# Experts of a mixture-of-experts layer: four at a time in four column groups of the array, on unsplit fp32 weights

## The chip, the cores and the metric

One core of one Trainium2 chip runs the whole program in one launch. The metric is the device time of one execution in microseconds. Before the change the median of 3 runs is 1587.62 us (1587.09 to 1587.66). The profile is one further execution of the same kernel.

## What is computed

A small network on 256 tokens of width 1024, all in fp32. A first block has a mixer (gated linear attention and block attention), attention over a memory, and a mixture of experts; after it come two layers of another kind (differential and stick-breaking attention, then a feed-forward part). The change lies in the mixture of experts. Each token picks one of 4 groups, and in it 2 of 8 experts, so 32 experts share 512 token places:

```
hid = silu(xb @ w_gate[e]) * (xb @ w_up[e])
return (hid @ w_down[e]) * w[:, None]
...
out = zeros((T, D)).at[buf_t].add(yb)
```

Here xb are the tokens of expert e. w_gate and w_up are 32 x 1024 x 512, w_down is 32 x 512 x 1024: 6 MB of fp32 for an expert, 201.3 MB for all, and every byte is used once.

## The kernel before

Nearly all large products run on fp32 weights split into two parts of the type fp32r. A weight chunk is 128 partitions x 1024 elements (512 KB). `load` (line 276) issues its transfer from SP's queue, `high` (L286, instruction L288) rounds it to fp32r on ScalarE, and `low` (L291, instruction L293) takes the difference on VectorE, or now and then on GpSimd. In the other layers `dense` (L317) multiplies three combinations of high and low parts (L327).

The expert stage begins at L706 with the buffers. `raws` (L713) is a ring of places that hold chunks: 16 buffers of `moeraw`, the idle tiles `kTc`, `vc`, `hBl`, `hAl`, `hAh`, `hBh`, the four buffers of `wraw`, two of `Y` once, and `gain`. Loads are issued in program order; SP waits at each for its buffer. The first four chunks are requested while the product before the stage still runs (L812), the next 25 ahead of the stage (`EARLY`, L896), the rest as the stream consumes them.

The routing (L855 to L885) works on VectorE: largest values, their positions, and the place of each token in its expert's list of 32 slots. Between its operations the splits of the first chunks are issued (L794, and L868 and L869 with the low parts on GpSimd). `select` (L922) makes a 0/1 matrix of tokens and slots for four experts, and `take` (L928) multiplies the rows of x by it in fp32, which gives the chosen tokens transposed. `put` (L937) writes them as a high part on ScalarE and a low part on VectorE. Each expert has 64 columns: 32 slots of high part and 32 of low part; 128 stationary columns hold one expert and a zero block or the neighbour.

A unit is two experts. `up` (L1059) streams the chunks of gate and up weights: per chunk the high and the low split, then 2 x 2 matmuls of 128 x 512 (`parts`, L1010, instruction L1015). The high and low rows of the result are added up by a product with a constant matrix (`comb`, L1070), which also transposes it. `hidden` (L1072) applies the gate and splits again. `down` (L1093) streams the down weights the same way. `weights` (L1034) multiplies the selection by the routing weights on GpSimd (L1039) and transposes it, and `scatter` (L1101) adds the weighted rows back to x for two units at a time (L1106, L1110). The order of chunks is up(0), up(1), down(0), up(2), down(1), and so on to down(15). Side work is put on an agenda that is counted in chunks (`at`, `tick`, L907 to L916).

After unit 10 (`OVER`) comes a branch for experts with more than 32 tokens (`overflow`, L1133, the branch itself L1138). All engines go through it. Loads of some chunks are issued before it, into places that the branch doesn't use.

At the end the last units are added up in PSUM (`add`, L1128, L1131), the result is normed and transposed (L1234 to L1298), and the next layer starts with L327.

Of the kernel before, what the change touches and what calls it, by code (L numbers as in the profile page):

```python
# [20 lines left out]
P = 128  # L21
# [6 lines left out]
MOE_RAW = 16  # L28
LAG = 3
POOLED = (4, 24, 3)  # L30
EARLY = 25
PAST = 16
OVER = 10
GAINS = 8
SECOND = 7
SHARES = 8
WARM = (2, 4)
ADDS = 2
# [13 lines left out]
ADDX = (2, 5, 3, 7)  # L52
# [13 lines left out]
def make_consts():  # L66
# [13 lines left out]
    e, r = np.arange(64)[None, :] // 32, np.arange(64)[None, :] % 32  # L80
    cols["comb"] = ((s // 64 == e) & (s % 32 == r)).astype(f)
# [27 lines left out]
GROUPS = (("ident", "ones", "before", "comb", "slots", "index", "down_from", "order"), ("tri16", "bucket"),  # L109
# [5 lines left out]
def forward(ctx: ExitStack, tc: tile.TileContext, a: dict, out: bass.AP):  # L115
# [595 lines left out]
    around = places[:-1] + shared, places[-1:]  # L711
# [5 lines left out]
    def nextraw():  # L717

        return next(v for v in raws if not closing or v[0] is not big or v[1] in ("kTc", "vc"))

    wg, wu, wd = a["w_exp_gate"][0], a["w_exp_up"][0], a["w_exp_down"][0]
    ahead, ready = collections.deque(), collections.deque()

    def halved(i, h, eng=nc.vector):
        ready.append((h, low(first[i], h, KC, 512, keep, eng)))

    with tc.tile_pool(name="crossp", bufs=1, reuse_waits="tile") as cp:
# [56 lines left out]
        def feed_moe(src, t, half):  # L784
# [8 lines left out]
            if half and t == 0:  # L793
                halved(0, high(first[0], KC, 512, keep))  # L794
# [16 lines left out]
        first = []  # L811
        add_to_x(slices(oT), a["w_co"][0], feed_moe, lambda: first.extend(  # L812
            load([wg[0, k0 * P:(k0 + KC) * P, :]], KC, 512, *nextraw()) for k0 in range(0, KD, KC)))
# [54 lines left out]
    for i in range(1, 4):  # L868
        halved(i, high(first[i], KC, 512, keep), nc.gpsimd)  # L869
# [18 lines left out]
    UNITS = [(2 * u, 2 * u + 1) for u in range(16)]  # L888
    last = len(UNITS) - 1
    xs2 = []  # L890
    for u in range(2):
        xs2.append(new(mp, [P, KD, 3, 2, 32], F32R, name="xs%d" % u))
        if u == 0:
            wt = s3("wt", 32)
            upcoming = [W[e, k0 * P:(k0 + KC) * P] for i in range(2) for e in UNITS[i] for W in (wg, wu) for k0 in range(0, KD, KC)]
            ahead.extend(load([src], KC, 512, *nextraw()) for src in upcoming[len(first):][:EARLY])  # L896
    hs2 = []
    for v in xs2:
        nc.gpsimd.memset(v[:, :, 1].bitcast(F32), 0.0)
    comb = cst("comb")  # L900
# [21 lines left out]
    def select(u):  # L922

        sel = sels[u] = new(mp2, [P, NT, 4, 32], name="sel")
        keep(tt(sel, key[:, :, 2 * u:2 * u + 4].rearrange("p t (e o) -> p t e o", o=1).to_broadcast([P, NT, 4, 32]),  # L925
                slots[:, None, None, :].to_broadcast([P, NT, 4, 32]), op=ALU.is_equal))

    def take(u, k0):  # L928

        ps = new(pst, [P, 4, 2, 2, 32], name="tp")  # L930
        for k in range(4):
            for t in range(NT):
                keep(mm(ps[:, k].rearrange("p u e r -> p (u e r)"), xr[:, t, (k0 + k) * P:(k0 + k + 1) * P],
                        sels[u][:, t].rearrange("p e r -> p (e r)"), start=(t == 0), stop=(t == NT - 1)))
        return ps

    def put(k0, ps, units=(0, 1)):  # L937
        views = [(xs2[i][:, k0:k0 + 4, 0::2], ps[:, :, i]) for i in units]
        for v, src in views:
            keep(nc.scalar.copy(v[:, :, :, 0], src))  # L940
        for v, src in views:
            keep(tt(v[:, :, :, 1], src, v[:, :, :, 0].bitcast(F32), op=ALU.subtract))

    def gather(u, first, step, lag):
        select(u)
        for i in range(2):
            at(first + step * i, lambda k0: at(lag, put, k0, take(u, k0)), 4 * i)
# [62 lines left out]
    def parts(xf, e, nk, last, acc, W, col):  # L1010

        def go(k0, ww):
            for i in range(2):
                for k in range(KC):
                    keep(mm(acc, xf[:, k0 + k, e * 64:e * 64 + P], ww[i][:, k],  # L1015
                            start=(e == 0 and k0 == 0 and i == 0 and k == 0),
                            stop=(e == last and k0 + KC == nk and i == 1 and k == KC - 1)))

        return [(W[k0 * P:(k0 + KC) * P, col:col + 512], functools.partial(go, k0)) for k0 in range(0, nk, KC)]

    def stream(chunks):
        for src, go in chunks:
            if ready:
                go(ready.popleft())
            else:
                raw = ahead.popleft() if ahead else load([src], KC, 512, *nextraw())
                h = high(raw, KC, 512, keep)
                go((h, low(raw, h, KC, 512, keep, nc.gpsimd if clock[0] < POOLED[1] and clock[0] % POOLED[0] == POOLED[2] else nc.vector)))
            tick()

    def flat(v):
        return v.rearrange("p k a b c -> p k (a b c)")

    def weights(u):  # L1034

        sel = sels[u - u % 2][:, :, u % 2 * 2:u % 2 * 2 + 2]
        selw = new(mp2, [P, NT, 2, 2, 32], name="selw")
        for d in range(2):
            nc.gpsimd.tensor_tensor(selw[:, :, :, d], sel,  # L1039
                                    wt[:, :, 2 * u:2 * u + 2].rearrange("p t (e o) -> p t e o", o=1).to_broadcast([P, NT, 2, 32]),  # L1040
                                    op=ALU.mult)
        ps = new(psm, [P, 512], name="mm")

        def turn():
            for t in range(NT):
                nc.tensor.transpose(ps[:, t * P:(t + 1) * P], selw[:, t].rearrange("p e d r -> p (e d r)"), ident)
            at(LAG, read)

        def read():
            sT[u] = new(mp, [P, T], name="selT", bufs=4)  # L1050
            keep(nc.scalar.copy(sT[u], ps[:, 0:T]))

        at(2, turn)

    def up_chunks(u, G=None, U=None):
        return [c for e, x_ in enumerate(UNITS[u]) for acc, W in ((G, wg), (U, wu))
                for c in parts(flat(xs2[u % 2]), e, KD, len(UNITS[u]) - 1, acc, W[x_], 0)]

    def up(u):  # L1059

        G, U = new(psm, [P, 512], name="mm"), new(psm, [P, 512], name="mm")
        at(2 if u else PAST, weights, u)
        stream(up_chunks(u, G, U))
        gu = [new(tmp, [P, 512], name="rows") for _ in range(2)]
        ps = new(psm, [P, 2, 4, 64], name="mm")

        def read(i, v):
            keep(nc.scalar.copy(gu[i], v))
            for k in range(4):
                keep(mm(ps[:, i, k], gu[i][:, k * P:(k + 1) * P], comb, start=True, stop=True))  # L1070

        def hidden():  # L1072
            if u < 2:
                hs2.append(new(mp, [P, 4, 3, 2, 32], F32R, name="hs%d" % u))
                nc.gpsimd.memset(hs2[u][:, :, 1].bitcast(F32), 0.0)
            hs = hs2[u % 2]
            hid = new(mp2, [P, 4, 64], name="hid")
            keep(nc.scalar.activation(hid, ps[:, 0], AF.Sigmoid))
            keep(nc.vector.tensor_mul(hid, hid, ps[:, 0]))
            keep(nc.vector.tensor_mul(hid, hid, ps[:, 1]))  # L1080
            hv = hid.rearrange("p k (e r) -> p k e r", e=2)
            keep(nc.scalar.copy(hs[:, :, 0::2, 0], hv))
            keep(tt(hs[:, :, 0::2, 1], hv, hs[:, :, 0::2, 0].bitcast(F32), op=ALU.subtract))

        at(LAG - 4, read, 0, G)
        at(LAG, read, 1, U)
        at(LAG + 2, hidden)

    def down_chunks(u, Y=(None, None)):
        return [c for e, x_ in enumerate(UNITS[u]) for half in range(2)  # L1090
                for c in parts(flat(hs2[u % 2]), e, 4, len(UNITS[u]) - 1, Y[half], wd[x_], half * 512)]

    def down(u):  # L1093

        Y = [new(psa, [P, 512], name="at") for _ in range(2)]
        stream(down_chunks(u, Y))
        Yg[u] = new(mp, [P, 2, 512], name="Y", bufs=2)
        for half in range(2):
            at(LAG - 2 + 2 * half, lambda *v: keep(nc.scalar.copy(*v)), Yg[u][:, half], Y[half])

    def scatter(units, first, step, lag):  # L1101
        def piece(t, half):
            hs = slice(half * 512, (half + 1) * 512)
            ps = new(pst, [P, 512], name="tp")
            for i, u in enumerate(units):
                mm(ps, sT[u][:, t * P:(t + 1) * P], Yg[u][:, half], start=(i == 0), stop=(i == len(units) - 1))  # L1106
# [447 lines left out]
```

## Time and profile before

| What | Value |
|---|---|
| median of 3 runs | 1587.62 us |
| the profiled execution's own time | 1591.64 us |
| its span, first to last instruction | 1590.0 us |
| mean granted TensorE clock | 0.989 |
| PE busy | 1532.9 us (96%), 7099 instructions |
| DVE busy | 1190.1 us (75%), 1498 instructions |
| ACT busy | 992.1 us (62%), 1353 instructions |
| POOL busy | 199.8 us (13%), 95 instructions |
| read from HBM | 381.10 MB |

The page lists busy times of the engines, then the span in 40 slices of 39.75 us, the queues of transfers, the chain that ended last, and groups of like instructions. PE is the TensorE matmul, PEld its weight load, DVE is VectorE, ACT ScalarE, POOL GpSimd, and SPq the queue from which SP issues loads. Matmul ends are modelled and overlap, so a busy PE is not a PE at its peak; distances between starts say more. In rows of the timeline the columns are the start in us, the duration in us, the engine, the line, the operation, the output and inputs, the shape, the count, and in brackets the idle time before and what ended it.

### The profile page before, as it was taken

The page shows a single profiled execution, that of the slowest core. Times are in us where ns is not written, and L with a number is a line of the kernel's source. Part 1 is how long each engine was busy: PE and PEld are TensorE (multiplying, and loading weights), DVE is VectorE, ACT ScalarE, POOL GpSimd, SP SyncE. Part 2 cuts the span into 40 slices and gives each one's busy share as a digit, 9 for nine tenths or more (in the row PEclk, how much of TensorE's full clock was granted, in tenths as well). Part 3 has the DMA queues.
Part 4 walks back from the last instruction along what each step waited for, and adds up shares of the span by engine and source line. Part 5 has one row for each costly group of instructions (what it writes and reads, how often), then busy time and mean ns, then how long its engine had stood idle before and what let it go on. Part 6 is the DMA issues. An engine that isn't in the chain of part 4 may idle for free. (4 is left out here: it accounts for less than half of the span.)

```text
span 1590.0 us, 20604 instructions
## 1 busy us (share of the span) xinstructions
PE 1532.9 (96%) x7099; PEld 1194.5 (75%) x7099; DVE 1190.1 (75%) x1498; ACT 992.1 (62%) x1353; POOL 199.8 (13%) x95
## 2 busy tenths in 40 slices
PE   7999999699999999999999999999999999999998
PEld 5778887466776767767667887888888887888886
DVE  5665575789999999999887876766656876766654
ACT  5455554579878887797774666555544566455543
POOL 1110000434335141142001000000000000000000
PEclk9999999899999999999999999999999999999999
DMA  8645559689999999999956545566567545566653
GB/s 283 218 137 160 182 173 375 209 295 370 386 387 387 386 387 340 341 386 386 387 187 195 147 141 164 182 189 186 185 186 220 168 137 152 178 195 186 184 187 106
DMA packets 220348, 383.59 MB, mean 241 GB/s; under 512 B 13464, under 2 KB 60000, under 8 KB 219856
## 3 DMA queue, kind: packets, MB, share of 16 engines
q1 hardware_dynamic: 217584, 373.76, 70.2%
q0 software_dynamic: 1648, 6.84, 1.4%
q10 hardware_dynamic: 1008, 1.64, 0.3%
q8 instruction: 57, 0.93, 0.2%
q14 instruction: 51, 0.42, 0.1%
HBM read 381.10 MB, written 2.65 MB: 241 GB/s over the span
## 5 line engine op out<-in xcount | busy, mean ns | idle before, releaser
L293 DVE TENSOR_TENSOR wl<-raw,wh 128x1024 fp32r<-128x1024 f32 x599 | 718.0, 1227 | 239.6 <-ACT wh L288 226.1
L288 ACT ACTIVATE wh<-raw 128x1024 fp32r<-128x1024 f32 x606 | 624.0, 1057 | 303.2 <-PE mm L327 258.9
L1015 PE MATMUL mm<-wl,xs 128*128 128x512 f32 x512 | 186.4, 446 | 8.6 <-DVE wl L293 5.5
L1039 POOL TENSOR_TENSOR selw<-sel,wt 128x128 f32<-128x128 f32 x32 | 139.7, 4385 | 272.9 <-DVE sel L925 187.6
L1015 PE MATMUL mm<-wh,xs 128*128 128x512 f32 x512 | 164.0, 403 | 0.6 <-ACT wh L288 0.6
L1015 PEld LDWEIGHTS mm<-wl,xs 128*128 128x128 f32 x512 | 91.3, 192 | 66.2 <-DVE wl L293 32.8
L327 PE MATMUL mm<-wh,hAl 128*128 128x512 f32 x424 | 139.1, 409 | 0.0
L327 PE MATMUL mm<-wh,hAh 128*128 128x512 f32 x424 | 134.3, 397 | 2.7 <-ACT wh L288 2.7
L327 PE MATMUL mm<-wl,hAh 128*128 128x512 f32 x424 | 134.3, 398 | 0.0
L327 PE MATMUL mm<-wl,hBh 128*128 128x512 f32 x424 | 133.3, 394 | 0.0
L327 PE MATMUL mm<-wh,hBl 128*128 128x512 f32 x424 | 132.4, 393 | 0.1
L327 PE MATMUL mm<-wh,hBh 128*128 128x512 f32 x424 | 132.1, 393 | 0.0
L1015 PEld LDWEIGHTS mm<-wh,xs 128*128 128x128 f32 x512 | 97.0, 191 | 27.2 <-ACT wh L288 3.7
L1015 PE MATMUL at<-wl,hs 128*128 128x512 f32 x256 | 89.4, 430 | 7.9 <-DVE wl L293 7.9
L327 PEld LDWEIGHTS mm<-wh,hAh 128*128 128x128 f32 x424 | 79.3, 190 | 19.8 <-ACT wh L288 3.1
L1015 PE MATMUL at<-wh,hs 128*128 128x512 f32 x256 | 87.2, 422 | 5.4 <-ACT wh L288 5.3
L327 PEld LDWEIGHTS mm<-wl,hAh 128*128 128x128 f32 x424 | 79.4, 190 | 17.2
L327 PEld LDWEIGHTS mm<-wh,hBh 128*128 128x128 f32 x424 | 78.9, 188 | 17.6
L327 PEld LDWEIGHTS mm<-wh,hBl 128*128 128x128 f32 x424 | 78.5, 188 | 18.0 <-issue 1.4
L327 PEld LDWEIGHTS mm<-wl,hBh 128*128 128x128 f32 x424 | 78.5, 188 | 16.9 <-issue 0.3
L327 PEld LDWEIGHTS mm<-wh,hAl 128*128 128x128 f32 x424 | 75.3, 191 | 12.3 <-issue 0.8
L1015 PEld LDWEIGHTS at<-wl,hs 128*128 128x128 f32 x256 | 45.1, 188 | 34.9 <-DVE wl L293 21.9
(482 smaller groups left out, 2245.5 us busy)
## 6 DMA issues: line engine op xcount, KB each, us to landing
raw<-in_w_in_dram SPq DMA_DIRECT2D x121, 512.0 KB, 3.7
raw<-in_w_exp_down_dram SPq DMA_DIRECT2D x101, 512.0 KB, 10.8
raw<-in_w_exp_gate_dram SPq DMA_DIRECT2D x95, 512.0 KB, 10.8
raw<-in_w_exp_up_dram SPq DMA_DIRECT2D x93, 512.0 KB, 10.8
raw<-in_w_ffn_in_dram SPq DMA_DIRECT2D x176, 256.0 KB, 3.2
raw<-in_w_ffn_out_dram SPq DMA_DIRECT2D x44, 512.0 KB, 3.8
raw<-in_w_out_dram SPq DMA_DIRECT2D x24, 512.0 KB, 3.8
raw<-in_w_ckv_dram SPq DMA_DIRECT2D x8, 512.0 KB, 3.9
```

The costliest lines, as they stand in the source:

```text
L288: order(nc.scalar.activation(h[:, :kc], raw[:, :kc], AF.Copy))
L293: order(eng.tensor_sub(l[:, :kc], raw[:, :kc], h[:, :kc].bitcast(F32)))
L327: order(mm(ps[t][:, :n], xs[k0 + k][part][:, t * P:(t + 1) * P], ww[:, k, :n], start=(k0 == 0 and i == 0 and k == 0), stop=(k0 + kc == nk ...
L1015: keep(mm(acc, xf[:, k0 + k, e * 64:e * 64 + P], ww[i][:, k], start=(e == 0 and k0 == 0 and i == 0 and k == 0), stop=(e == last and k0 + K ...
L1039: nc.gpsimd.tensor_tensor(selw[:, :, :, d], sel, wt[:, :, 2 * u:2 * u + 2].rearrange("p t (e o) -> p t e o", o=1).to_broadcast([P, NT, 2, ...
```

## The change

Four experts are worked on at once, each in 32 of the array's 128 columns, with the unsplit fp32 weights times 32 unsplit slots. The split of expert weights, their low parts on VectorE and GpSimd, the high and low slots, and the product with `comb` go. For gate and up weights a partition now takes two neighbouring rows (a 4 KB run) where it took two rows that lie 128 apart (two runs of 2 KB), and `take` picks the columns of x to match; for down weights a chunk is 128 whole rows of 4 KB, but in the last group two halves as before. The ring gains the eight buffers of the split parts (`whi`, `wlo`) and one of `moeraw`; 34 loads are issued ahead instead of 25. The branch comes after group 5 of 8. GpSimd multiplies the selection once per group. Lags between steps are shorter, and `put` is one copy.

```diff
-MOE_RAW = 16
+MOE_RAW = 17
...
-EARLY = 25
-PAST = 16
-OVER = 10
...
+EARLY = 34
+OVER = 5
...
+    def load_rows(src, pool=wraw, tag="raw"):
+
+
+        raw = new(pool, [P, KC, 512], name=tag, **({"bufs": 2} if tag == "Y" else {}))
+        nc.sync.dma_start(out=raw.rearrange("p k n -> p (k n)"), in_=src.rearrange("(p k) n -> p (k n)", p=P))
+        return raw
...
-    around = places[:-1] + shared, places[-1:]
+    halves_of = [(whi, "wh")] * 4 + [(wlo, "wl")] * 4
+    around = places[:-1] + shared + halves_of, places[-1:]
...
-            if half and t == 0:
-                halved(0, high(first[0], KC, 512, keep))
...
-    for i in range(1, 4):
-        halved(i, high(first[i], KC, 512, keep), nc.gpsimd)
...
+    def take(g, k0):
+
+        ps = new(pst, [P, 4, GROUP * 32], name="tp")
         for k in range(4):
             for t in range(NT):
...
+                first = (k0 + k) // KC * KC * P + k % KC
+                keep(mm(ps[:, k], xr[:, t, first:first + KC * (P - 1) + 1:KC],
+                        sels[g][:, t].rearrange("p e r -> p (e r)"), start=(t == 0), stop=(t == NT - 1)))
...
+    def put(g, k0, ps):
+        keep(nc.scalar.copy(xsT[g % 2][:, k0:k0 + 4], ps))
+
+    def gather(g, first):
+        at(first, select, g)
         for i in range(2):
...
+            at(first + 1 + i, lambda k0: put(g, k0, take(g, k0)), 4 * i)
+        at(first + 3, weights, g)
...
+    def stream(quads):
+
+        for srcs, go in quads:
+            go([ahead.popleft() if ahead else fetch(src, nextraw()) for src in srcs])
+            tick()
...
+    def weights(g):
+
+        selw = new(mp2, [P, NT, GROUP, 32], name="selw")
+        nc.gpsimd.tensor_tensor(selw, sels[g], wt[:, :, GROUP * g:GROUP * (g + 1)].rearrange("p t (e o) -> p t e o", o=1).to_broadcast([P, NT, GROUP, 32]),
+                                op=ALU.mult)
...
+        at(1, turn)
+
+    def up_quads(g, G=None, U=None):
+        def quad(acc, W, k0):
+            def go(ww):
                 for k in range(KC):
...
+                    for j, w in enumerate(ww):
+                        keep(mm(acc[strip(j)], xsT[g % 2][:, k0 + k, strip(j)], w[:, k],
+                                start=(k0 + k == 0), stop=(k0 + k == KD - 1), skip_group_check=True))
+            return of_group(g, W, slice(k0 * P, (k0 + KC) * P)), go
...
+    def up(g):
+
+        G, U = new(psm, [P, 512], name="mm"), new(psm, [P, 512], name="mm")
+        stream(up_quads(g, G, U))
+        hid = new(tmp, [P, 512], name="rows")
+        keep(nc.scalar.activation(hid, G, AF.Sigmoid))
+        keep(nc.vector.tensor_mul(hid, hid, G))
+        keep(nc.vector.tensor_mul(hid, hid, U))
...
+    def down_quads(g, Y=(None, None)):
+        def whole(k):
+            def go(ww):
+                for half in range(2):
+                    for j, w in enumerate(ww):
+                        keep(mm(Y[half][strip(j)], hT[g][:, k, strip(j)], w[:, half], start=(k == 0), stop=(k == 3), skip_group_check=True))
+            return of_group(g, wd, slice(k * P, (k + 1) * P)), go
...
+        if g == OVER:
+
+            coming = [src for srcs, _ in down_quads(g - 1) + up_quads(g + 1) for src in srcs]
+            free_of = [v for v in itertools.islice(raws, len(places) + len(shared) + len(halves_of)) if v not in shared]
+            ahead.extend(fetch(src, v) for src, v in zip(coming, free_of))
             overflow()
```

`strip(j)` is the slice of partitions or columns from 32 j to 32 j + 32, and `of_group(g, W, rows)` the four experts' pieces of W. A quad is the four chunks that go together.

## Rows read from the trace of the kernel before

**Rows 1.** The page's 40 slices: busy tenths of PE, GB/s of all transfers.
```profile
PE   7999999699999999999999999999999999999998
...
GB/s 283 218 137 160 182 173 375 209 295 370 386 387 387 386 387 340 341 386 386 387 187 195 147 141 164 182 189 186 185 186 220 168 137 152 178 195 186 184 187 106
```

**Rows 2.** Stretches: length, busy PE, PEld, DVE, ACT, POOL; clock, DMA share, GB/s.
```profile
290.00:318.00 28.00, 22.02 (x90) 16.58 (x91) 19.89 (x28) 15.74 (x21) 8.27 (x4) 0.87 0.59 187
...
397.00:600.00 203.00, 196.99 (x871) 143.96 (x870) 195.29 (x200) 168.72 (x208) 73.24 (x12) 1.00 1.05 386
600.00:637.00 37.00, 36.12 (x170) 25.76 (x169) 34.89 (x37) 29.15 (x38) 7.28 (x4) 1.00 0.89 326
637.00:680.00 43.00, 41.27 (x189) 30.18 (x188) 39.39 (x44) 34.45 (x46) 5.02 (x2) 1.00 0.97 353
...
810.00:830.00 20.00, 18.22 (x65) 11.47 (x63) 15.93 (x16) 16.29 (x22) 0.00 (x0) 1.00 0.27 84
```

**Rows 3.** Timeline of the load queue: first and last issues of expert chunks.
```profile
238.03 3.10 SPq L282 DMA_DIRECT2D raw<-in_w_exp_gate_dram  x4
...
246.09 4.39 SPq L282 DMA_DIRECT2D raw<-in_w_exp_gate_dram  x4
251.47 4.72 SPq L282 DMA_DIRECT2D raw<-in_w_exp_up_dram  x4
...
784.21 11.46 SPq L282 DMA_DIRECT2D raw<-in_w_exp_down_dram  x9
```

**Rows 4.** Timeline from the last expert matmul to the next layer's first, TensorE.
```profile
825.87 0.62 PE L1015 MATMUL at<-wl,hs 128*128 128x512 f32 x2
...
835.18 0.70 PE L327 MATMUL mm<-wh,hAh 128*128 128x512 f32 x2
```

**Rows 5.** The page's groups: busy us and mean ns of the split and of POOL's weights.
```profile
L293 DVE TENSOR_TENSOR wl<-raw,wh 128x1024 fp32r<-128x1024 f32 x599 | 718.0, 1227 | 239.6 <-ACT wh L288 226.1
L288 ACT ACTIVATE wh<-raw 128x1024 fp32r<-128x1024 f32 x606 | 624.0, 1057 | 303.2 <-PE mm L327 258.9
...
L1039 POOL TENSOR_TENSOR selw<-sel,wt 128x128 f32<-128x128 f32 x32 | 139.7, 4385 | 272.9 <-DVE sel L925 187.6
```

**Rows 6.** Timeline of the routing and the first expert matmul.
```profile
280.34 0.22 DVE L863 TENSOR_TENSOR oha<-at,mia 128x64 f32<-128x64 f32 x1
...
280.97 4.68 POOL L293 TENSOR_TENSOR wl<-raw,wh 128x1024 fp32r<-128x1024 f32 x2 [0.20 <-ACT wh L288]
281.11 2.32 DVE L860 TENSOR_TENSOR at<-em,mb 128x64 f32<-128x64 f32 x1
...
286.02 2.26 DVE L863 TENSOR_TENSOR ohb<-at,mib 128x64 f32<-128x64 f32 x1
...
290.60 5.87 PE L933 MATMUL tp<-sel,xr 128*128 128x128 f32 x32 [0.86 <-DVE sel L925]
...
296.23 0.72 PE L1015 MATMUL mm<-wh,xs 128*128 128x512 f32 x2
```

**Rows 7.** Timeline of fp32 passes: full width (weight loads), then two strips of 64 columns.
```profile
279.33 0.19 PEld L782 LDWEIGHTS at<-gain,c_ident 128*128 128x128 f32 x1 [0.24 <-issue]
...
281.48 0.19 PEld L782 LDWEIGHTS at<-gain,c_ident 128*128 128x128 f32 x1 [0.24 <-issue]
...
929.80 0.65 PE L1462 MATMUL tp<-aw,sv 128*64 128x256 f32 x4
930.28 0.39 PE L1464 MATMUL tp<-aw,sv 128*64 128x128 f32 x4
930.60 0.74 PE L327 MATMUL mm<-wh,hBl 128*128 128x512 f32 x2
```

**Rows 8.** Stretches with transfers in long runs; last column GB/s.
```profile
1217.50:1219.50 2.00, 2.00 (x10) 1.66 (x9) 2.00 (x6) 0.53 (x2) 1.61 (x1) 1.00 1.02 410
...
1217.00:1220.00 3.00, 3.00 (x15) 2.47 (x14) 2.75 (x6) 1.03 (x3) 1.61 (x1) 1.00 1.00 406
```

**Rows 9.** Waits of the load queue in 600 to 690: us in total, times, longest.
```profile
SPq L282 <- PEq L1138: 12.5, 1, 12.5
```

More of the change, by code (lines that the diff above doesn't have):

```diff
@@ L717, in nextraw @@
     def nextraw():
-        return next(v for v in raws if not closing or v[0] is not big or v[1] in ("kTc", "vc"))
+        return next(v for v in raws if not closing or v not in halves_of and (v[0] is not big or v[1] in ("kTc", "vc")))
     wg, wu, wd = a["w_exp_gate"][0], a["w_exp_up"][0], a["w_exp_down"][0]
-    ahead, ready = collections.deque(), collections.deque()
-    def halved(i, h, eng=nc.vector):
-        ready.append((h, low(first[i], h, KC, 512, keep, eng)))
+    ahead = collections.deque()
     with tc.tile_pool(name="crossp", bufs=1, reuse_waits="tile") as cp:
@@ L885, in forward @@
     keep(stt(key, am.bitcast(F32), -1000.0, pk, op0=ALU.mult, op1=ALU.add))
[L888 to L893, printed above, removed]
-            wt = s3("wt", 32)
[L895 to L900, printed above, removed]
+    xsT = []
+    for g in range(2):
+        xsT.append(new(mp, [P, KD, GROUP * 32], name="xs%d" % g))
+        if g == 0:
+            wt = s3("wt", 32)
+            ahead.extend(load_rows(src, *nextraw()) for src in upcoming[GROUP:][:EARLY])
+    hT = {}
     slots = cst("slots")
@@ L1021, in stream @@
[L1021 to L1032, printed above, removed]
@@ L1055, in up_chunks @@
[L1055 to L1068, printed above, removed]
-            for k in range(4):
[L1070 to L1093, printed above, removed]
+    def stream(quads):
+        for srcs, go in quads:
+            go([ahead.popleft() if ahead else fetch(src, nextraw()) for src in srcs])
+            tick()
+    def fetch(src, place):
+        return load(src, KC, 512, *place) if isinstance(src, list) else load_rows(src, *place)
@@ L1095, in down, with scatter @@
+    def down(g):
         Y = [new(psa, [P, 512], name="at") for _ in range(2)]
-        stream(down_chunks(u, Y))
-        Yg[u] = new(mp, [P, 2, 512], name="Y", bufs=2)
+        stream(down_quads(g, Y))
+        Yg[g] = new(mp, [P, 2, 512], name="Y", bufs=2)
         for half in range(2):
-            at(LAG - 2 + 2 * half, lambda *v: keep(nc.scalar.copy(*v)), Yg[u][:, half], Y[half])
-    def scatter(units, first, step, lag):
+            keep(nc.scalar.copy(Yg[g][:, half], Y[half]))
+    def scatter(g, first):
@@ L1181, in forward @@
     select(0)
[L1182 to L1190 removed]
+    for k0 in (0, 4):
+        put(0, k0, take(0, k0))
+    for _ in shares():
+        pass
+    at(2, weights, 0)
+    at(4, spread, past_slots())
+    for g in range(last + 1):
+        if g == last:
             closing.append(True)
[L1192 removed]
             gf, g12 = xr[:, 0], xr[:, 1]
@@ L1225, in forward @@
     for i, v in enumerate(both):
-        at(ADDS + i, add, *v, last - 1)
-    chunks = down_chunks(last, Y)
-    stream([chunks[i] for i in (0, 1, 4, 5, 2, 3, 6, 7)])
+        at(1 + i // 2, add, *v, last - 1)
+    stream(down_quads(last, Y))
     flush()
```

134 lines of the change are left out of this document (51 added, 83 removed).

## The prediction

> **What bounds the kernel now.** I read the slices of the page first, then the stretches of the expert stage, then the queue that issues its loads, then the rows of the operations that the change replaces. In the slices [rows 1] PE is at 9 nearly throughout, so they alone don't say what an edit in the expert stage is worth. The stretches do [rows 2]. Three things are full at once in 397 to 600 us: PE 197.0 of 203.0 us busy, DVE 195.3, and the transfers at 386 GB/s with a DMA share of 1.05. 386 GB/s is what loads in 2 KB runs reach at their best here, so this middle is set by DMA, and DVE is hardly behind. It is not so at the edges: 187 GB/s in 290 to 318, 326 and 353 on the two sides of 637, and in 810 to 830 there are 84 GB/s while PE still works off what has landed. So the stage is a stream of 384 chunks of 512 KB, and the time is the stream's pace plus the time in which something else holds it up.
>
> The load queue gives the frame [rows 3]. The first expert chunk is issued at 238.03 us, the ninth at 246.09; from there issues go at the landing pace (the next four-chunk row starts 5.38 us later: 1.35 us each), with eight chunks in flight, so the ninth issue marks the first landing, 246.1. If nothing held the stream up, the last chunk would land at 246.1 + 383 x 1.358 (524,288 bytes at 386 GB/s) = 766 us. In fact nine chunks are issued from 784.21 on at that pace, so the last is issued near 795 and lands some eight paces later, about 806 (784.21 + 8 x 1.358 + 8 x 1.358). Forty us of the stream are lost, and the last expert matmul ends only at 826.5 [rows 4], 20 us after the landing. The next layer's first matmul starts at 835.18.
>
> **The change, part by part.**
>
> *No split of expert weights.* Each chunk costs ACT 1.06 us and DVE 1.23 us [rows 5], 384 times: up to 407 and 470 us of work. Neither engine is on the new path; what this buys is that buffers come free when PE has read them. That is what removes the losses at the edges, where the 187 GB/s stand beside buffers full of chunks that wait to be split.
>
> *No split on POOL before the first expert.* Beside POOL's pieces (from 280.97 on) three small DVE operations of the routing take 2.3 us each (the first 2.32, the last 2.26 [rows 6]), while their like just before takes 0.22. Without POOL they should be short again: 3 x (2.29 - 0.22) = 6.2 us. The first expert matmul then comes at 296.23 - 6.2, about 290. Picking stays 16 fp32 matmuls (32 records, 5.87 us).
>
> *Matmuls.* An fp32 matmul of 512 columns is two passes; six weight loads of such passes start from 279.33 to 281.48, 0.43 us apart [rows 7]. The new kernel has per group of four experts 24 steps of k (8 for gate, 8 for up, 4 x 2 for down), each of four strips x two passes. If four strips go at once, a step costs two passes, 0.86 us, and I take 0.90 for their staggered starts. The nearest row has two strips of 64 columns: eight passes, four of 256 and four of 128 columns, begin at 929.80 and the next full-width matmul begins at 930.60 [rows 7]. One after the other they need 4 x 0.215 + 4 x 0.107 = 1.29 us, ideally paired 0.64; they take 0.80. So two strips do go together; four are not shown. Bounds for a step: 0.86 us, and 8 x 0.43 = 3.44 if strips go singly. I take 0.90: 24 x 0.90 = 21.6 us per group, plus picking 5.9 [rows 6], the scatter's four matmuls at 0.86, 3.4, and six transposes at 0.18 (a record of the picking), 1: 32 us per group at the full clock, against 48 chunks x 1.295 = 62 us of transfers. PE is half idle and DMA alone sets the pace.
>
> *Loads in 4 KB runs.* No long stretch has them alone. The nearest, 1217 to 1220 us, mixes 4 and 8 KB runs: 406 GB/s, its best 2 us 410 [rows 8]. Bounds: 386 (runs gain nothing) and 410. I take 405, 1.295 us per chunk, because the nearest rows lie there. The last group's down weights keep 2 KB runs: 16 x 0.063 = 1 us more.
>
> [...]
>
> *Buffers and the start.* 17 + 3 + 3 + 4 + 8 + 2 + 1 = 38 chunks can be loaded before a matmul frees one. The 38th lands at 246.1 + 37 x 1.295 = 294; the first four buffers come free near 292. I charge 1 us, between 0 and 8 (first step at half clock, 87% granted in 290 to 318 [rows 2]).
>
> *The join of the overflow branch.* Now SP waits there 12.5 us for PE [rows 9]; with eight chunks in flight this costs some 10 us in two stretches (37 x (1 - 326/386) = 5.8 and 43 x (1 - 353/386) = 3.7 [rows 2]). After the change 29 chunks are issued ahead of it, PE waits there for SP rather than the reverse, and then frees buffers faster than they fill. I charge 3, between 0 and 10.
>
> *A wait that is added.* The selection weights now take POOL one multiply per group over 256 elements instead of two per pair of experts over 128; at 4.39 us for 128 [rows 5] that is 8.8 us, and PE's transposes of them stand one quad of loads behind it instead of two chunks. PE then waits up to 8.8 us, with the strips of the next quads queued behind it; for those waits the release of buffers, and for that SP. It costs nothing while buffers are free: eight chunks in flight alone cover 10 us, and in the first group three quads have freed twelve buffers before it, 15 us. The shares of group 0 are worked out in one go before the stream, on DVE and ACT behind the first picks, and PE doesn't wait for them. SP passes only the loads.
>
> *Sum.* Last landing 246.1 + 383 x 1.295 + 1 (2 KB) + 1 (start) + 3 (join) = 747. The last landing's eight strips are two steps, 1.8 us: 749 for the last expert matmul, against 826.5. From there to the next layer's first matmul it is 8.7 us now; I add 4 us (between 0 and 8), because PE comes from a half-idle stretch, perhaps at a lower clock, and because the next layer's first chunks now land and are split inside this tail instead of before it. Gain 77.5 - 4 = 73.5 us. Against the profiled execution's own 1591.64 that gives 1518; the median of the runs is 4 us lower, 1587.62, so **1514 us**.
>
> **Rivals.**
>
> *Longer runs gain nothing*: the transfers are already at their rate with 2 KB runs. Pace 1.358: last landing 766 + 4 = 770, end 772, gain 54.5 - 4: **1537**. For it: 386 is steady over 203 us. Against: 406 to 410 in the stretch of long runs. Chance 0.13. [...]
>
> *PE paces in places.* [...] Chance 0.10.
>
> *Strips go one after another* (the change doesn't do what it says). A step costs 3.44 us, 192 x 3.44 + 8 x 10.3 = 743 us from 290: the last expert matmul at 1033, 206 us later than now, and 4 for the tail: **1798**. It decides from (826.5 - 290 - 82) / 192 = 2.4 us per step, that is when fewer than 1.5 strips run at once. Against it: the pairs above. For it: no row has four strips or 32 columns. Chance 0.05.
>
> **How the numbers follow.** The forecast has 0.72. With every unknown at its good end (410 GB/s, no charges, no longer tail) the last landing is 736, the gain 89: 1499. With 386 GB/s, 10 us at the join and 8 in the tail: 1548. The range 1499 to 1545 takes in the first rival and most of the second; left out are strips that go singly, a clock that stays low, and extremes together. A measurement here can tell about 0.2%, 3 us, from no change. Faster 0.94, same 0.01, slower 0.05: all cases but the strips one after another lie well under 1584.
>
> **What would show it.** Right: no ACT or DVE split between 290 and 745; the slices at 400 GB/s or above without a gap from 250 to 745; load issues 1.29 us apart; four strips starting within some tens of ns; PE near half busy in the stretch; the three DVE operations of the routing at 0.2 to 0.3 us; the last expert landing near 747 and the last expert matmul within 3 us of it. Wrong: issues 1.355 us apart (the runs); SP waiting on PE for long while PE is full (strips or clock); a hole of 10 us or more at the branch; more than 13 us from the last expert matmul to the next layer's first.

## The result and the profile after

| What | Before | After |
|---|---|---|
| median of 4 runs | 1587.53 us | 1506.33 us (1505.91 to 1507.26) |
| ratio, 95% interval | | 0.9487 (0.9476 to 0.9499) |
| the profiled execution's own time, span | 1591.64, 1590.0 us | 1506.5, 1504.8 us |
| mean granted TensorE clock | 0.989 | 0.995 |
| last expert matmul ends | 826.5 us | 742.3 us |
| from there to the next layer's first matmul | 8.69 us | 8.69 us |

The kernel is 81.2 us faster. The page of the changed kernel, with busy times, the 40 slices (37.62 us each) of PE, and the GB/s, against [rows 1]:

```profile
PE 1435.1 (95%) x6795; PEld 938.1 (62%) x6795; DVE 723.1 (48%) x1054; ACT 593.2 (39%) x881; POOL 42.2 (3%) x59
...
PE   7999999999898998899899999999999999999998
...
GB/s 289 237 133 135 198 174 316 387 410 409 409 409 409 409 409 409 408 409 409 339 215 151 137 161 159 216 184 183 188 176 229 140 150 161 171 205 182 185 193 99
```

DVE does 467 us less, ACT 399 us less. The slices of PE hardly changed; those of the transfers did: eleven in a row at 408 to 410, where before 386 or 387 stood, with two slices at 340 and 341. The stretches, columns as in [rows 2]:

```profile
238.00:290.00 52.00, 48.71 (x255) 36.48 (x256) 25.28 (x71) 20.44 (x47) 2.58 (x4) 0.97 1.01 398
290.00:318.00 28.00, 27.60 (x240) 11.47 (x233) 4.25 (x13) 4.38 (x7) 2.99 (x5) 1.00 0.98 381
397.00:600.00 203.00, 183.70 (x771) 47.97 (x772) 13.38 (x21) 13.15 (x24) 1.84 (x3) 1.00 1.03 409
600.00:637.00 37.00, 30.94 (x160) 10.11 (x161) 3.78 (x6) 2.04 (x4) 3.47 (x4) 0.91 1.03 408
637.00:680.00 43.00, 38.89 (x151) 8.02 (x152) 2.06 (x3) 2.93 (x5) 0.51 (x1) 1.00 1.03 409
```

In 290 to 318 the transfers rose from 187 to 381 GB/s, and on the two sides of 637 from 326 and 353 to 408 and 409. DVE and ACT have 13 us of work in 203 where they had 195 and 169. The load queue's timeline, against [rows 3]:

```profile
237.88 17.03 SPq L281 DMA_DIRECT2D raw<-in_w_exp_gate_dram  x16
...
282.77 0.33 SPq L281 DMA_DIRECT2D gain<-in_w_exp_gate_dram  x1
289.89 5.89 SPq L281 DMA_DIRECT2D raw<-in_w_exp_gate_dram  x9
...
720.19 10.12 SPq L273 DMA_DIRECT2D raw<-in_w_exp_down_dram  x8
```

The ninth issue, which waits for the first landing (in 237 to 247 the queue waits twice for loads of `w_exp_gate`, 1.9 us in all), comes at 245.67, and the last expert chunk is issued at 729.67 (before: 795.05). All places are full from 282.77 to 289.89 (no issue between), the one long stop of the stream; no other gap between two issues of expert chunks is over 3.5 us. TensorE's timeline at the end, against [rows 4]:

```profile
740.44 1.90 PE L1070 MATMUL at<-raw,hs 128*32 128x512 f32 x10 [0.31 <-DMA raw<-in_w_exp_down_dram]
742.27 1.98 PE L1112 MATMUL mm<-Y,selT 128*128 128x512 f32 x4
...
751.03 0.71 PE L325 MATMUL mm<-wh,hAh 128*128 128x512 f32 x2
```

The strips of the last chunk begin as it lands, at 740.44, and are done 1.9 us later; before, TensorE was 20 us behind the last landing. In TensorE's timeline of the middle a chunk's strips start every 1.28 us, each released by its transfer:

```profile
525.49 1.04 PE L1063 MATMUL at<-gain,hs 128*32 128x512 f32 x2 [0.23 <-DMA gain<-in_w_exp_down_dram]
526.77 1.04 PE L1063 MATMUL at<-raw,hs 128*32 128x512 f32 x2 [0.23 <-DMA raw<-in_w_exp_down_dram]
528.05 0.62 PE L1063 MATMUL at<-raw,hs 128*32 128x512 f32 x1 [0.23 <-DMA raw<-in_w_exp_down_dram]
528.06 0.62 PE L1063 MATMUL at<-wl,hs 128*32 128x512 f32 x1
528.07 0.62 PE L1063 MATMUL at<-gain,hs 128*32 128x512 f32 x1
```

Three chunks of a quad run the two passes of their first half alone as they land; when the fourth lands (528.05), its first half goes beside the second halves of the other three, one in each column group, within 0.02 us and from four different buffers. TensorE waits for transfers, not the reverse: in 238 to 745 the load queue's waits for L1034's matmuls add up to 12.0 us.

### The profile page after: what moved, and what is told of

It reads as the page before. It is cut to its first block, busy times and chain, and to the rows that moved or that the text cites. A ratio compares the mean times of both kernels' runs of the same rounds, so it can differ in the third digit from the quotient of the medians.

```text
span 1504.8 us, 18303 instructions
## 1 busy us (share of the span) xinstructions
PE 1435.1 (95%) x6795; PEld 938.1 (62%) x6795; DVE 723.1 (48%) x1054; ACT 593.2 (39%) x881; POOL 42.2 (3%) x59
## 5 line engine op out<-in xcount | busy, mean ns | idle before, releaser
L291 DVE TENSOR_TENSOR wl<-raw,wh 128x1024 fp32r<-128x1024 f32 x317 | 387.0, 1224 | 265.0 <-ACT wh L286 251.7
L286 ACT ACTIVATE wh<-raw 128x1024 fp32r<-128x1024 f32 x317 | 335.0, 1059 | 286.1 <-PE mm L325 254.8
L1034 PE MATMUL mm<-raw,xs 128*32 128x512 f32 x636 | 145.1, 603 | 10.1 <-DMA raw<-in_w_exp_gate_dram 5.4
L1092 DVE TENSOR_TENSOR x<-x,tp 128x512 f32<-128x512 f32 x24 | 16.5, 688 | 268.9 <-PE tp L1091 268.9
L1063 PE MATMUL at<-raw,hs 128*32 128x512 f32 x276 | 85.1, 603 | 11.2 <-DMA raw<-in_w_exp_down_dram 11.2
L1034 PEld LDWEIGHTS mm<-raw,xs 128*32 128x32 f32 x636 | 28.3, 109 | 97.3 <-issue 34.8
L932 ACT COPY xs<-tp 128x512 f32<-128x512 f32 x16 | 9.4, 585 | 165.3 <-PE tp L927 165.3
L1063 PEld LDWEIGHTS at<-raw,hs 128*32 128x32 f32 x276 | 14.4, 108 | 68.5 <-DMA raw<-in_w_exp_down_dram 55.9
L325 PE MATMUL mm<-wh,gTl 128*128 128x512 f32 x176 | 54.6, 391 | 0.0
L325 PE MATMUL mm<-wh,gTh 128*128 128x512 f32 x176 | 54.4, 390 | 0.0
```

Source lines behind the costliest of these rows:

```text
L286: order(nc.scalar.activation(h[:, :kc], raw[:, :kc], AF.Copy))
L291: order(eng.tensor_sub(l[:, :kc], raw[:, :kc], h[:, :kc].bitcast(F32)))
L325: order(mm(ps[t][:, :n], xs[k0 + k][part][:, t * P:(t + 1) * P], ww[:, k, :n], start=(k0 == 0 and i == 0 and k == 0), stop=(k0 + kc == nk ...
L932: keep(nc.scalar.copy(xsT[g % 2][:, k0:k0 + 4], ps))
L1034: keep(mm(acc[strip(j)], xsT[g % 2][:, k0 + k, strip(j)], w[:, k], start=(k0 + k == 0), stop=(k0 + k == KD - 1), skip_group_check=True))
L1063: keep(mm(Y[half][strip(j)], hT[g][:, k, strip(j)], w[:, half], start=(k == 0), stop=(k == 3), skip_group_check=True))
```

## The experiments

Each ratio is to the kernel before, whose median beside these runs was 1587.6 to 1588.2 us. The changed kernel's time is 1506.3 us.

### Which half of the change gives what

**The changed kernel with 2 KB runs** (down weights always in column halves, `take` without its stride):

```diff
-        nc.sync.dma_start(out=raw.rearrange("p k n -> p (k n)"), in_=src.rearrange("(p k) n -> p (k n)", p=P))
+        nc.sync.dma_start(out=raw, in_=src.rearrange("(k p) n -> p k n", p=P))
...
-        if g < last:
-            return [whole(k) for k in range(4)]
```

> The changed kernel with its expert loads in 2 KB runs again (gate and up rows 128 apart, down weights in column halves), all else kept. Theory (the stream of chunks sets the time): the pace goes from 1.283 back to about 1.356 us per chunk, 383 x 0.073 = 28 us, so about 1534 us, with the stretch 397 to 600 at 386 GB/s. Rival (the gain is TensorE's, run length does not matter): 1506 us.

Measured: 1532.7 us, ratio 0.9652 (0.9636 to 0.9669). Its stretches (columns as above) and the end of its stream on TensorE:

```profile
290.00:318.00 28.00, 27.59 (x242) 11.78 (x238) 3.33 (x10) 4.63 (x8) 2.48 (x5) 1.00 1.05 386
397.00:600.00 203.00, 178.05 (x739) 45.08 (x740) 14.08 (x22) 11.41 (x21) 1.85 (x3) 0.99 1.05 386
...
637.00:680.00 43.00, 38.68 (x186) 11.10 (x178) 3.78 (x6) 3.21 (x6) 3.99 (x4) 0.98 1.05 386
```

```profile
766.71 1.90 PE L1069 MATMUL at<-raw,hs 128*32 128x512 f32 x10 [0.30 <-DMA raw<-in_w_exp_down_dram]
```

386 GB/s from end to end: same rate as before in the middle, and nothing lost at the edges. The last chunk lands at 766.7, where the prediction put an unhindered stream of 2 KB runs at 766. So the change without its longer runs is worth 1587.5 - 1532.7 = 54.8 us, and the longer runs 26.4 on top. The 54.8 us are not the end of the split alone: this kernel also has 38 places for chunks where the kernel before had 29, an earlier branch, shorter lags and a plainer `put`. The run with eight buffers fewer, below, has 30 places and loses 10 us, so the extra places are a small part; the lags and `put` were not tried by themselves.

**The kernel before with 4 KB runs**, split kept (the last unit's down weights in 2 KB runs):

```diff
+    def load_rows(src, pool=wraw, tag="raw"):
+        raw = new(pool, [P, KC, 512], name=tag, **({"bufs": 2} if tag == "Y" else {}))
+        nc.sync.dma_start(out=raw.rearrange("p k n -> p (k n)"), in_=src.rearrange("(p k) n -> p (k n)", p=P))
...
+        def whole(e, k):
+            def go(ww):
+                for half in range(2):
+                    for i in range(2):
+                        keep(mm(Y[half], flat(hs2[u % 2])[:, k, e * 64:e * 64 + P], ww[i][:, half],
```

> The kernel before with 4 KB runs for the expert weights (the last two experts' down weights excepted), split and all else kept. Theory (TensorE and VectorE stand right behind the loads there, 197 and 195 of 203 us busy): the pace can gain at most some 3% in the 310 us that were bound by loads, so about 1578 us. Rival (run length alone carries the gain of the pace): 28 us less, 1560 us.

Measured: 1610.1 us, ratio 1.015 (1.0126 to 1.0174): slower by 1.5%, where both theories had it faster. Its transfers run at 374 GB/s in 397 to 600, below 2 KB runs. One thing stands out among ScalarE's groups: the copy of a unit's result waits 23.1 us in 290 to 850 (last column: idle before, and what ended it), and in the kernel before not at all. With whole rows both halves of Y end with the last chunk; with column halves the first is ready half a unit earlier. Two kernels tested this, one with the copy a chunk later, one with 4 KB runs for gate and up weights alone:

```diff
-            at(LAG - 2 + 2 * half, lambda *v: keep(nc.scalar.copy(*v)), Yg[u][:, half], Y[half])
+            at(LAG - 1 + half, lambda *v: keep(nc.scalar.copy(*v)), Yg[u][:, half], Y[half])
```

> The kernel before with 4 KB runs, its copy of the first half of Y requested two chunks after the end of a unit's down weights instead of one (the second half: three, as before). Theory: what made the kernel before slower with whole rows is not the transfers but ScalarE, which stands in its queue at the copy of Y until TensorE has done the unit's last chunk (23.1 us of idle time before L1120 in 290 to 850, about 1.45 us for each of 16 units, against 0.0 in the kernel before, whose first half of Y was ready half a unit earlier), with the splits of the next chunks queued behind it. One chunk later the wait should fall to about 0.3 us: 16 x 1.1 = 18 us less than 1610, so about 1592. Rival: the splits' chain is the bound either way and the wait only shows it; then about 1608 to 1610.

```diff
-        if u == last:
+        if u <= last:
             return [([src], go) for e, x_ in enumerate(UNITS[u]) for half in range(2)
```

> The kernel before with 4 KB runs for gate and up weights alone; down weights in column halves of 2 KB runs as before. Theory: the copy of Y is what cost the 22 us, so with halves it costs nothing again, and 256 chunks can land up to 0.075 us sooner each (19 us); but VectorE's split, 1.14 us from start to start plus its other work, is close behind the transfers, so only part of it shows: about 1580, between 1570 and 1588. Rival: long runs or the strided picking hurt the split kernel by themselves: 1600 or more.

Measured: 1596.6 us (ratio 1.0055, 1.0039 to 1.0072) and 1590.1 us (1.0014, 1.0005 to 1.0024). ScalarE's group of Y copies in 290 to 850, first with whole rows, then a chunk later:

```profile
L1120 ACT COPY Y<-at 128x512 f32<-128x512 f32 x30 | 17.5, 582 | 23.1 <-PE at L1108 23.1
```

```profile
L1120 ACT COPY Y<-at 128x512 f32<-128x512 f32 x30 | 17.5, 583 | 6.5 <-PE at L1108 6.5
```

The wait fell by 16.6 us, the time by 13.5, so that queue is most of the 22 us lost. With gate and up weights alone it is gone, and still nothing is gained, though two thirds of the bytes come in 4 KB runs. The stretch 397 to 600 of that kernel:

```profile
397.00:600.00 203.00, 196.99 (x875) 144.84 (x875) 195.23 (x201) 168.50 (x209) 73.97 (x13) 1.00 1.02 395
```

DVE is as busy as before (195.2 of 203) and the load queue now waits for DVE's splits (L299) 290 us in 238 to 850, where the kernel before had 149 for the like (L293). The loads run at 395 GB/s here instead of 386, but then stand longer at the branch (240 GB/s in 600 to 637, against 326), and the last chunk is issued only 3.8 us sooner (791.27 against 795.05). So the chain behind the loads, the split and the products that read it, was a second bound at least as near as the transfers: in this kernel longer runs alone bought nothing. TensorE is busy 197.0 of 203 us in both kernels, and in this one its weight loads wait 17.7 us of that stretch for DVE's split; which of the two sets the pace of that chain no run separates. I had allowed for 1570 to 1588; part of the loss at whole rows (the 6.5 us of waiting that remained) was not looked into further.

### What the column groups are worth

**All four experts on the full width**, so that no two products run at once:

```diff
-                        keep(mm(acc[strip(j)], xsT[g % 2][:, k0 + k, strip(j)], w[:, k],
+                        keep(mm(acc, xsT[g % 2][:, k0 + k], w[:, k],
```

> The changed kernel with all four experts' products on the full width of the array (128 stationary columns, one accumulator), so that no two can run side by side; the instruction count, loads and waits are the same. It adds up the four experts' products where the changed kernel keeps them apart. Theory: a chunk is then four passes of 0.43 us in a row, 1.72 us against a landing every 1.283 us, and TensorE sets the pace: 384 x 1.72 = 660 us, and about 10 us per group for picking, scatter and transposes, from 288: last expert matmul near 1030 instead of 742, time about 1795. With the side work hidden in between: 1715. Rival: side-by-side strips are not what makes it possible, since passes of different experts overlap anyway: 1506 to 1560.

Measured: 1774.2 us, ratio 1.118 (1.1161 to 1.1199). Stretch and timeline of TensorE:

```profile
397.00:600.00 203.00, 203.00 (x534) 94.92 (x533) 10.30 (x16) 9.05 (x17) 1.23 (x2) 1.00 0.83 282
```

```profile
502.98 16.47 PE L1063 MATMUL at<-raw,hs 128*128 128x512 f32 x38
```

38 passes in 16.47 us: 0.43 us apart, without a gap, and the transfers fall to 282 GB/s. Without the column groups the unsplit fp32 product would have made the kernel 186 us slower than before.

**Two column groups of 64**, experts 0 and 2 in one, 1 and 3 in the other:

```diff
-                        keep(mm(acc[strip(j)], xsT[g % 2][:, k0 + k, strip(j)], w[:, k],
+                        keep(mm(acc[pair(j)], xsT[g % 2][:, k0 + k, pair(j)], w[:, k],
```

with `pair(j)` the slice of 64 from 64 (j % 2).

> The changed kernel with two column groups of 64 instead of four of 32: experts 0 and 2 of a quad use columns 0 to 63, experts 1 and 3 columns 64 to 127. It adds up two experts' products where the changed kernel keeps them apart. Theory: only 1.34 strips have to run at once (four passes of 0.43 us per chunk against a landing every 1.283 us), and two do: 1506 to 1510. Rival: four column groups are needed, since passes of one group wait for each other and hold up the queue behind them: 1560 or more.

Measured: 1509.3 us, ratio 0.9505 (0.949 to 0.9519); in 397 to 600 PE is busy 198.25 of 203 us at 409 GB/s. Two at once are enough to within 3 us (the ratio's interval overlaps the changed kernel's), as four passes of 0.43 us against a landing every 1.283 us need 1.34.

**Expert by expert**: all steps of a chunk first, then the next expert's.

```diff
-                for k in range(KC):
-                    for j, w in enumerate(ww):
+                for j, w in enumerate(ww):
+                    for k in range(KC):
```

> The changed kernel with the matmuls of a quad ordered expert by expert instead of step by step, so that the two steps of one expert, which share a column group, stand next to each other and only one pass in four meets another column group. Theory (concurrent strips are what keeps TensorE under the loads): 12 pass slots of 0.43 us, 5.16 us per quad, plus 10 us per group for the rest: 290 + 96 x 5.16 + 82 = 867 us for the last expert matmul instead of 742, so about 1631 us. Rival (strips run one by one as their chunks land anyway, concurrency buys nothing): 1506 us.

Measured: 1509.8 us, ratio 0.95 (0.9484 to 0.9516): the theory's price was some 120 us too high. Its timeline of TensorE shows why, first at the start, where four chunks lie ready, then in the middle:

```profile
298.25 0.62 PE L1034 MATMUL mm<-raw,xs 128*32 128x512 f32 x1
298.26 0.62 PE L1034 MATMUL mm<-kTc,xs 128*32 128x512 f32 x1
298.27 0.62 PE L1034 MATMUL mm<-vc,xs 128*32 128x512 f32 x1
298.29 0.62 PE L1034 MATMUL mm<-hBl,xs 128*32 128x512 f32 x1
298.70 0.59 PE L1034 MATMUL mm<-raw,xs 128*32 128x512 f32 x1
...
525.16 0.62 PE L1063 MATMUL at<-gain,hs 128*32 128x512 f32 x1
525.19 0.59 PE L1063 MATMUL at<-wl,hs 128*32 128x512 f32 x1
525.61 1.02 PE L1063 MATMUL at<-gain,hs 128*32 128x512 f32 x2
526.43 0.62 PE L1063 MATMUL at<-raw,hs 128*32 128x512 f32 x1
526.47 0.59 PE L1063 MATMUL at<-gain,hs 128*32 128x512 f32 x1
```

At 298.25 the first passes of all four chunks start within 0.04 us, ahead of the first chunk's second pass (298.70), though the kernel's text has all four passes of a chunk before the next chunk's; the last of the sixteen begins at 299.60. So this order does not keep the strips apart. The expectation's premise, that only one pass in four meets another column group, was wrong, and the run doesn't price concurrency; the full-width run does. In the middle each chunk starts 1.27 us after the one before, the pace at which chunks land (1.283 us), and its own four passes are 0.43 us apart. PE is busy 203.0 of 203.0 us there and the stream is still at 409 GB/s.

**Last expert first**: the order in a quad turned round in the three loops, so that TensorE waits for all four chunks and then does 16 passes at once.

```diff
-                    for j, w in enumerate(ww):
+                    for j, w in reversed(list(enumerate(ww))):
```

> The changed kernel with the four experts of a step taken in reverse order, so that TensorE waits for the last chunk of a quad and then runs its eight strips four at a time: 1.8 us of work in 5.1 us. Theory: no change of time, 1506 us within 2, busy TensorE in 397 to 600 us falling from 90% to about 50%. Rival (a half-idle TensorE gets a lower granted clock, and the tail pays): granted clock under 0.9 in the stretch and 4 us more, 1510 us.

Measured: 1505.8 us, ratio 0.948 (0.9464 to 0.9495). A quad in its timeline of TensorE, and its stretch:

```profile
536.65 1.92 PE L1034 MATMUL mm<-raw,xs 128*32 128x512 f32 x16 [1.73 <-DMA raw<-in_w_exp_gate_dram]
541.68 3.48 PE L1034 MATMUL mm<-raw,xs 128*32 128x512 f32 x16 [3.10 <-DMA raw<-in_w_exp_gate_dram]
```

```profile
397.00:600.00 203.00, 129.56 (x770) 37.64 (x774) 13.39 (x21) 12.58 (x23) 1.85 (x3) 0.85 1.03 409
```

Sixteen passes in 1.92 us are four times four: side by side they take what four take in one strip (3 x 0.43 + 0.62 = 1.91 us). TensorE idles for a third of the time (busy 64%, where I had expected about 50%), the granted clock drops to 0.85 (the same 16 passes take 3.48 us after a wait of 3.10 us), and the time is the same. The half of the rival that names the clock came true, its 4 us did not: TensorE has that much slack here.

### The start, the join and the end

**GpSimd busy beside the routing**: three subtractions of 128 x 1024 at its start, as the split had there before.

```diff
+    xs1 = new(mp, [P, KD, GROUP * 32], name="xs1")
+    for i in range(3):
+        nc.gpsimd.tensor_sub(xs1.rearrange("p k n -> p (k n)"), x[:, 0], x[:, 1])
```

> The changed kernel with three subtractions of 128 x 1024 put on GpSimd at the start of the routing, into a buffer that is not used yet, as the split had there before; their result is not used. Theory: the small VectorE operations beside them take about 2.3 us again instead of 0.22, the first strip comes about 6 us later (294), the buffers are full from 282.8 on, so the stream stands about 6 us longer: 1511 to 1513. Rival: the start is covered by the eight chunks in flight and by slack later: 1506 to 1507.

Measured: 1513.2 us, ratio 0.9527 (0.9511 to 0.9544): 6.8 us more than the changed kernel. The timeline of the routing, first the changed kernel, then this one; against [rows 6]:

```profile
279.40 0.23 DVE L861 TENSOR_TENSOR at<-lg,ma 128x64 f32<-128x64 f32 x1
...
284.02 4.01 PE L927 MATMUL tp<-sel,xr 128*128 128x128 f32 x32 [0.94 <-DVE e L944]
...
287.96 5.36 PE L1034 MATMUL mm<-raw,xs 128*32 128x512 f32 x48
...
290.43 0.66 POOL L1017 TENSOR_TENSOR selw<-sel,wt 128x256 f32<-128x256 f32 x1 [11.01 <-DVE wt L963]
```

```profile
279.37 7.18 POOL L871 TENSOR_TENSOR xs<-x 128x1024 f32<-128x1024 f32 x3
279.47 2.33 DVE L861 TENSOR_TENSOR at<-lg,ma 128x64 f32<-128x64 f32 x1
...
284.25 0.22 DVE L863 TENSOR_REDUCE mia<-at 128x8 f32<-128x64 f32 x1
284.38 0.15 DVE L863 TENSOR_REDUCE mig<-at 128x2 f32<-128x8 f32 x1
284.50 2.13 DVE L864 TENSOR_TENSOR oha<-at,mia 128x64 f32<-128x64 f32 x1
...
288.84 0.37 PE L883 MATMUL mm<-am,wr 128*128 128x32 f32 x1 [6.52 <-DVE am L880]
...
290.57 5.83 PE L930 MATMUL tp<-sel,xr 128*128 128x128 f32 x32 [0.94 <-DVE e L947]
```

Three rows of DVE's operations with two inputs take 2.33 (279.47), 2.46 (281.83, two operations) and 2.13 us (284.50), where the changed kernel has 0.23, 0.30 and 0.22, while the two reductions with one input at 284.25 and 284.38 take 0.22 and 0.15 us beside the third subtraction. The picking starts 6.55 us later (290.57) and takes 5.83 us instead of 4.01: TensorE has idled for 6.5 us shortly before it, and the granted clock is 0.64 in 290.4 to 296.3, and 1.00 in 283.9 to 288.0 of the changed kernel. First strip at 296.3 against 288.0, and the transfers of 290 to 318 fall from 381 to 271 GB/s, 28 x (381 - 271)/409 = 7.5 us of the stream.

**Eight buffers fewer:**

```diff
-MOE_RAW = 17
+MOE_RAW = 9
...
-EARLY = 34
+EARLY = 26
```

> The changed kernel with 9 buffers of moeraw instead of 17, and 26 loads issued ahead instead of 34: 30 places instead of 38. Theory: the first strip frees the first buffers at 288 whatever their number, so the load queue stands from about 272.5 instead of 282.8 on; now it stands 7.1 us and loses 1.9 us of transfers (381 GB/s against 409 in 290 to 318), so 5.2 us are covered by what is in flight; with 17.4 us of standing it should lose about 12, 10 more than now: 1516. Rival: the start is not on the path, or the loss is made up later: 1506 to 1508.

Measured: 1516.4 us, ratio 0.954 (0.9526 to 0.9555), as the theory has it. The last chunk is issued at 738.50 instead of 729.67. What stands between the full buffers and the first strip is paid for in the time: 10.1 us here.

**No overflow branch:**

```diff
             ahead.extend(fetch(src, v) for src, v in zip(coming, free_of))
-            overflow()
```

> The changed kernel without the branch for experts with more than 32 tokens; the loads issued ahead of it stay. It leaves out the overflow branch, which with this data does no work. Theory: the join costs nothing, since the transfers run at 409 GB/s through it: 1506, within 1 us. Rival, the prediction's charge: it costs 3 us of the stream: 1503.

Measured: 1505.0 us (1503.2 to 1506.4), ratio 0.9474 (0.9461 to 0.9487). The medians are 1.4 us apart with the ranges overlapping. With 409 GB/s in 600 to 637 against 408 with the branch, it is not the join that makes them: this kernel's first strip comes at 285.0 in the profiled execution instead of 288.0. That first strip, 3 us sooner, is as much as the two profiled executions differ (1503.15 and 1506.5). No sign of the charge of 3 us is left for the join.

**Whole rows in the last group too**, with the last expert first:

```diff
-        if g < last:
+        if g <= last:
             return [whole(k) for k in range(4)]
```

> The changed kernel with the last group's down weights as whole rows too (4 KB runs), and the experts of a quad taken from the last to the first. Theory: the last 16 chunks land in 1.283 us each instead of 1.355, so the last one lands 1.2 us sooner, and TensorE's strips wait for a quad's last chunk without cost; but both halves of Y end with the last chunk, so the tail after it has one more copy of 0.58 us in it: 1505 to 1506, about 0.5 us less than the changed kernel. Rival: the halves let the tail start half a group earlier, and without them it is 2 to 4 us longer: 1507 to 1509.

Measured: 1504.9 us (1502.3 to 1506.7), ratio 0.947 (0.9457 to 0.9483). The last issue comes 1.25 us sooner (728.42), but from the last strip to the next layer's first matmul it takes 10.0 us instead of 8.7. That is a wash within the spread; no variant is clearly better than the changed kernel.

## Why the prediction was right, and where its terms were off

The forecast was 1514 with 1499 to 1545; 1506.3 lies in it, and the mechanism is the one that was forecast: the stage is a stream of loads, and the time followed the last landing. The terms, each against what the runs showed:

- **What bounded the kernel before.** Right that 40 us of the stream were lost at the edges and 20 us lay behind the landing: without the split, at the same 386 GB/s, the stream lands at 766.7. The sentence "this middle is set by DMA, and DVE is hardly behind" was half right: with 4 KB runs for gate and up weights on the split kernel the loads rose to 395 GB/s and the time did not fall (1590.1 us), so the chain of split and products held as much as the transfers. The long runs' 26 us were measured only together with the unsplit product.
- **GpSimd's split beside the routing.** Right in kind (DVE's operations at 0.22 to 0.23 again), too small in size: 6.2 us were counted, the first strip came 8.3 us earlier (288.0 against 296.2). Missed was the slower picking behind TensorE's wait: in the kernel before TensorE waits 6.45 us, then picks in 5.87 us at a granted clock of 0.61 (0.50 in 290.6 to 294, 1.00 in 295 to 296.4), where the changed kernel needs 4.01 us at 1.00. The 0.87 of [rows 2] was read and not followed up.
- **Strips.** Four do go at once, a step in two passes 0.43 us apart (the prediction took 0.90 us for a step). Where the prediction had "PE is half idle", the page shows it busy 90% of the middle. That is the order of work, not need: strips run as their chunk lands, so single strips stretch TensorE's work over the whole quad, and turned round it is 64%. The sign in the profile that I had named ("PE near half busy") would have misled.
- **The pace.** 1.283 us per chunk (409 GB/s) instead of 1.295: 383 x 0.012 = 4.6 us, the largest term that was mis-sized. The short stretch at 410 GB/s [rows 8] was nearer than the value between. The rival that longer runs gain nothing had 386 for both; 386 and 409 speak against it.
- **Buffers and the start.** 1 us charged, 28 x (1 - 381/409) = 1.9 us lost; eight buffers fewer cost 10 us, as worked out from it before that run.
- **The join.** 3 us charged, nothing found. TensorE stands at the branch for 4.76 us, but 29 chunks had been issued ahead of it and the transfers run through, at 408 GB/s in 600 to 637.
- **The weights of the selection.** 8.8 us on GpSimd were expected to be covered; there was nothing to cover: 0.61 to 0.66 us for 256 elements. The 4.39 us of [rows 5] were no price of one multiply but the mean of 32 that took 0.40 to 19.04 us each (median 1.14), beside a DVE that is busy 195.3 of 203 us in the middle. Whether the busy DVE makes the long ones no run tests.
- **The tail.** 4 us charged, none seen: 8.69 us in both kernels. The strips run to the end of the stream, and the granted clock is 1.00 in 730 to 750.

The sum: the last landing came at 740.4 instead of 747, that is 4.6 of pace, 3 of the join and 0.4 of an earlier first landing, less 0.9 at the start and 0.1 in the last group (these add up to 7.0 where 6.6 were measured); with the 4 us of tail and 1.0 elsewhere in the program the gain between the two profiled executions is 73.5 + 6.6 + 4 + 1.0 = 85.1 us. The medians are only 81.2 apart, as the profiled execution of before was 4 us above its median, and in which stage those 4 us lay was not found. So the forecast was 11.6 us too cautious between the profiles, and 7.7 by the medians (1514 against 1506.3). Nearly all terms that were off erred to the same side; the figure is near because each was small.

The rivals: with 2 KB runs the time is 1532.7, where the first rival had 1537 (the tail again). The second, TensorE as the pace in places, the changed kernel does not show: the granted clock is 1.00 in 397 to 600, four strips start within 0.02 us, and the transfers stay at 409 GB/s. In the order that leaves TensorE idle the clock was 0.85 there and two steps (16 passes) took 3.48 us at 541.68, and it cost nothing (1505.8 us). Strips one after another give 1774, where 1798 was worked out; the side work is (1010.9 - 288 - 384 x 1.72)/8 = 8 us per group rather than 10.3.

## What to carry to other kernels

In the kernel before, transfers (386 GB/s) and a vector chain (DVE busy 195.3 of 203 us) were both near full in the same stretch, and faster loads alone (395 GB/s) showed nothing, 1590.1 us: in such a case compute for each alone how early the last item could be through, and expect the gain of the faster loads only together with the edit that frees the other. A mean of a group of like instructions is not a price before its spread is seen (here 0.40 to 19.04 us around a mean of 4.39). The fp32 products with few result rows became as fast as the loads when each had its own column group (1506.3 us, against 1774.2 on the full width), and two at once were enough to within 3 us, where pass time over landing time asks for 1.34. Price a small operation by a row where the engine beside it is idle if it will be idle (here 0.22 us, against some 2.3 beside GpSimd), and count with a wait of TensorE the slower work seen right behind it (here 5.83 us instead of 4.01).

## What the runs showed that I had not expected

- The loads run at 386 GB/s in 2 KB runs (in 397 to 680 of the changed kernel with 2 KB runs) and at 408 to 410 in 4 KB runs (eleven slices of 37.62 us), both steady for hundreds of us.
- Passes in different column groups overtake each other: in the run expert by expert the first passes of four chunks start within 0.04 us, ahead of a pass of the first chunk that stands before them in the kernel's text. In the run with the last expert first, where the first passes of a quad take its last chunk and wait for it (1.73 us), all sixteen start after that wait and take 1.92 us.
- Beside GpSimd's three subtractions (7.18 us in all, 2.4 each) operations with two inputs that take 0.22 or 0.23 us in the changed kernel take 2.13 and 2.33 on DVE, two in a row 2.46, and reductions with one input still 0.15 to 0.22.
- After a wait of 6.5 us the same 32 picking passes take 5.83 us at a granted clock of 0.64, and 4.01 at 1.00 in the changed kernel, without that wait.
